# A planner that tracks every tile, and low weight halves kept in HBM, in a hybrid recurrent decoder step

## The chip, the cores and the metric

The kernel runs on one core of a Trainium2 chip. The metric is device time in microseconds for one execution. Three runs of the kernel before gave 3065.84, 3066.15 and 3074.48 us, median 3066.15. 

## The reference

One layer of a recurrent decoder, on 2048 prompt tokens and 32 sample tokens, model width 1024, all in float32:

```python
h = layernorm(x, emb_ln_g, emb_ln_b)
u = h @ w_in                       # 31 groups of 128 columns, for four mixers
y = concat(gated_deltanet(u), mamba2_ssd(u), hgrn2(u), mlstm(u))   # A, B, C, D
h1 = layernorm(alpha * h + y @ w_out, ln1)
out = layernorm(alpha * h1 + relu(h1 @ w_up) ** 2 @ w_down, ln2)   # d_ff 4096
```

The four mixers are causal recurrences. They are computed in chunks: inside a chunk by small matmuls with decay masks (A also solves a unit triangular system), and from chunk to chunk through a state matrix per head. The outputs are the tokens and all the final states.

## The kernel before

**Tiling.** The 2048 prompt tokens are four blocks of 512; the 32 sample tokens ride along in block 0 of the first projection and in block 2 of what follows, as 544 columns in two pieces of 272. The stages in PE's order: P(0) to P(3), the product with `w_in`; W(0), the product with `w_out`, placed inside P(3); then F(0) to F(3), the feed-forward part, with W(1) to W(3) inside the end of F(0) to F(2).

**Weight units.** A weight unit is 128 output columns by 512 rows, 256 KB. There are 832 in PE's order: 62 in each P, 16 in each W, 128 in each F (136 in F(3), where the last units are used twice for half the columns). Every float32 product is made of three passes in the faster `float32r` type: weights and activations are split into a high half (rounded) and a low half (the rest), and PE computes high x high, low x high and high x low. So a unit of 512 columns is 12 matmuls on PE, one of 544 columns 24. The weights are loaded again for every block, and split again: `wraw` is the load, ACT makes `whi` by a copy (`cpv`), and POOL or DVE makes `wlo = wraw - whi` (`w_split`, engine chosen by `tvp`). `w_pump`, called ahead of each unit, keeps loads up to five units ahead and splits up to three ahead. `wraw`, `whi` and `wlo` have four buffers each.

**Side chains.** Beside the products, the kernel weaves in generators: the evacuation and convolution of each group of `u` (`u_gen`), layer norms (`ln0`, `ln1`, `ln2`), loads of the mixers' output for `w_out` (`y_pre`), and two long state chains, `ma` for mixer A (PSUM tiles `pa`) and `mb` for B, C and D (PSUM tiles `pb`), 16 prompt chunks and one sample chunk in each. Every `yield` in such a generator ends a step; the next step's instructions are issued when the planner thinks that its inputs are ready. `R.tick`, called after every three product matmuls (six of 272 columns), decides.

**The planner.** The order of all engines is fixed when the program is built. `_Run` keeps a clock for each engine; `_Eng` wraps the engines and calls `cost` for each instruction. For an instruction of a side chain, `cost` lets it start at the latest of the engine's clock, the step's start, and the end of the chain's previous instruction, whatever that one touched. A DMA costs 0.55 us on SP's clock and is taken to land 2.5 us later. Buffers are not looked at. A step is issued when the chain's ready time is not more than `SLACK` = 0.03 us past PE's clock, and while DVE's and ACT's clocks are not over 2 us ahead of PE's.

**Queues.** Each engine takes its instructions in order, and a waiting one holds those behind it. All DMAs go out from SP's queue, in order as well. So a store that waits for its data, or a series of stores, holds the weight loads behind it.

## Time and profile before

| | |
|---|---|
| median of three runs | 3066.15 us |
| profiled run, span | 3058.42 us, 3056.6 us |
| PE busy, idle | 2889.3 us, 167.3 us |
| DVE, ACT, POOL busy | 2147.3, 1244.0, 1649.5 us |
| mean granted PE clock | 0.982 |
| moved by DMA | 407.10 MB, 133 GB/s on the mean |
| `wlo` made by POOL, by DVE | 740, 92 |
| last matmul of a state chain | 2396.9 us |

Stages begin at: P(0) 20.3 us, P(1) 260.0, P(2) 497.7, P(3) 732.1, F(0) 1041.4, F(1) 1603.0, F(2) 2175.6, F(3) 2672.1. The span runs from the first to the last instruction. PE's busy time is not its work alone: matmuls are pipelined, and where the granted clock is 0.5 they take twice as long and count as busy. All lines of the kernel's engine calls are one helper line (L253), DMAs another (L374), so groups are told apart by tiles.

### The profile page before, as it was taken

How to read it: one execution, taken by the hardware profiler on the slowest of the kernel's cores; microseconds unless marked ns; L12 is line 12 of the kernel's file. 1: busy time of each engine (PE TensorE's matmuls, PEld its weight loads, DVE VectorE, ACT ScalarE, POOL GpSimd, SP SyncE). 2: the span in 40 equal slices, each digit the busy share in tenths (PEclk: the TensorE clock that was granted, in tenths of full speed). 3: DMA queues.
4: the chain of work that ended last, by engine and by line, in shares of the span. 5: the costliest groups of instructions: out<-in, count | busy, mean ns of one | idle time of the engine just before them, and what ended most of it. 6: DMA issues, size and time to landing. Idle time of an engine off the chain costs nothing. (4 is left out here: it accounts for less than half of the span.)

```text
span 3056.6 us, 48030 instructions
## 1 busy us (share of the span) xinstructions
PE 2889.3 (95%) x16668; PEld 2484.1 (81%) x16668; DVE 2147.3 (70%) x4074; ACT 1244.0 (41%) x2645; POOL 1649.5 (54%) x1996
## 2 busy tenths in 40 slices
PE   7979999989999899999999999998989999999997
PEld 7978777778777688777877877888889999888886
DVE  6977887896986777777877766577787544474454
ACT  4654564654563533333344322233533222432222
POOL 5646775856665544654555536445363444444545
PEclk9989999999999999999999999999999999999999
DMA  6766465456466344454445424454333433333333
GB/s 189 97 180 183 119 197 174 123 153 200 108 166 185 116 135 129 130 162 126 141 127 145 128 85 139 125 167 138 108 120 108 130 90 89 110 117 97 97 95 98
DMA packets 361262, 407.10 MB, mean 133 GB/s; under 512 B 65468, under 2 KB 207804, under 8 KB 361020
## 3 DMA queue, kind: packets, MB, share of 16 engines
q1 hardware_dynamic: 361020, 404.04, 46.5%
q8 instruction: 132, 2.16, 0.3%
q14 instruction: 110, 0.90, 0.1%
HBM read 340.20 MB, written 63.72 MB: 132 GB/s over the span
## 5 line engine op out<-in xcount | busy, mean ns | idle before, releaser
L253 PE MATMUL pd<-g,whi 128*128 128x512 f32 (+2 forms) x8080 | 2238.4, 362 | 19.1 <-ACT g L253 8.8
L253 POOL TENSOR_TENSOR wlo<-wraw,whi 128x512 fp32r<-128x512 f32 x740 | 1040.3, 1413 | 1241.5 <-ACT whi L253 1074.1
L253 PEld LDWEIGHTS pd<-g,whi 128*128 128x128 f32 x8080 | 1393.9, 190 | 224.9 <-DVE g L253 10.9
L253 PE MATMUL pd<-g,wlo 128*128 128x512 f32 (+2 forms) x4040 | 1306.1, 354 | 14.7 <-POOL wlo L253 14.7
L253 PEld LDWEIGHTS pd<-g,wlo 128*128 128x128 f32 x4040 | 721.0, 191 | 107.1 <-POOL wlo L253 19.6
L253 ACT ACTIVATE whi<-wraw 128x512 fp32r<-128x512 f32 x795 | 487.6, 626 | 474.4 <-PE pd L253 254.9
L253 DVE TENSOR_TENSOR g<-g 128x512 fp32r<-128x512 f32 (+5 forms) x335 | 320.5, 961 | 171.7 <-ACT g L253 165.4
L253 ACT ACTIVATE g<-pd 128x512 f32<-128x512 f32 (+2 forms) x340 | 173.3, 528 | 533.6 <-PE pd L253 531.6
L253 DVE TENSOR_TENSOR g<-g,pd 128x512 f32<-128x512 f32 (+2 forms) x288 | 159.2, 570 | 209.1 <-PE pd L253 208.5
L253 ACT ACTIVATE g<-g 128x512 f32<-128x512 f32 (+4 forms) x358 | 218.8, 633 | 82.2 <-DVE g L253 46.9
L253 POOL TENSOR_TENSOR a<-nb,x 128x124 f32<-128x124 f32 (+30 forms) x496 | 193.5, 390 | 63.3 <-DMA nb<-ud32d 33.3
L253 POOL TENSOR_TENSOR x<-x,a 128x124 f32<-128x124 f32 (+30 forms) x496 | 193.8, 391 | 38.9
L253 DVE CAST g<-g 128x512 fp32r<-128x512 f32 (+1 forms) x154 | 157.8, 1025 | 25.5 <-POOL g L253 19.0
L253 POOL TENSOR_TENSOR g<-g 128x512 f32<-128x512 f32 (+3 forms) x83 | 121.7, 1472 | 36.9 <-ACT g L253 33.4
L253 ACT ACTIVATE b<-b 128x256 f32<-128x256 f32 (+3 forms) x201 | 81.2, 405 | 147.8 <-DVE b L253 147.1
L253 DVE TENSOR_TENSOR b<-laC 128x64 f32<-128x64 f32 (+2 forms) x474 | 125.2, 321 | 8.5 <-DMA laC<-UC 8.5
L253 DVE SCALAR_TENSOR_TENSOR g<-g,par 128x512 f32<-128x512 f32 (+1 forms) x128 | 124.8, 991 | 3.6 <-ACT g L253 3.6
L253 DVE SCALAR_TENSOR_TENSOR g<-g 128x512 f32<-128x512 f32 (+3 forms) x124 | 113.8, 926 | 7.2 <-ACT g L253 6.9
L253 DVE TENSOR_SCALAR g<-g 128x512 int32<-128x512 int32 (+7 forms) x137 | 86.9, 652 | 33.4 <-ACT g L253 32.5
L253 DVE TENSOR_TENSOR wlo<-wraw,whi 128x512 fp32r<-128x512 f32 x92 | 73.2, 796 | 52.6 <-ACT whi L253 52.1
L253 DVE TENSOR_TENSOR kzD<-laC,b 64x128 f32<-64x128 f32 (+1 forms) x228 | 103.1, 452 | 5.5 <-ACT b L253 3.9
L253 DVE BATCH_NORM_STATS2 bst<-g 128x6 f32<-128x512 f32 (+1 forms) x98 | 65.5, 680 | 40.5 <-ACT g L253 36.4
(2534 smaller groups left out, 2792.1 us busy)
## 6 DMA issues: line engine op xcount, KB each, us to landing
wraw<-in_w_dn_u_dram SPq DMA_DIRECT2D x264, 256.0 KB
wraw<-in_w_up_u_dram SPq DMA_DIRECT2D x256, 256.0 KB
wraw<-in_w_in_u_dram SPq DMA_DIRECT2D x248, 256.0 KB
nb<-ud32d SPq DMA_DIRECT2D x128, 256.0 KB
wraw<-in_w_out_u_dram SPq DMA_DIRECT2D x64, 256.0 KB
UC<-g SPq DMA_DIRECT2D x40, 256.0 KB
g<-in_x_prompt_dram SPq DMA_DIRECT2D x32, 256.0 KB
hTd<-g SPq DMA_DIRECT2D x32, 256.0 KB
```

The lines of the kernel that those rows point to most:

```text
L253: r = f(*a, **k)
```

## The change

**The planner** (`_Sim`, called by `_Run` and `_Eng`) records, for each tile, which part of it each instruction reads or writes, and when that ends. An instruction now starts when its own engine is free and the accesses that it really conflicts with have ended, with a delay per engine. A tile from a pool with 2 to 16 buffers starts when the accesses to the buffer's former tile have ended. DMAs take SP in order (0.42 us each), wait there for their data, share a wire priced by size, and land 1.6 us after. `SLACK` becomes -0.25.

**The low halves.** The first time a unit of `w_out`, `w_up` or `w_down` is split (for `w_in` the second time), the low half is also stored to HBM (`lod`), when the unit comes up on PE. Later blocks load it, right behind `wraw`, four units ahead of use, and do not compute it. `wraw` has three buffers now, `wlo` five. In the program, 206 halves are stored and 564 loaded; of the subtractions 240 stay on POOL and 28 on DVE. The number of PE's instructions is the same, and each side chain does the same steps.

**Starts.** `ln0(b)` starts when P(b-1) has reached unit group 8, and its stores of `hT` stand one to a step with paced early splits between them; `y_pre` waits until the end of the stage before is near; at the start, the fourth weight unit is loaded later.

```diff
-SLACK = 0.03
+SLACK = -0.25
+LN0_AT = 8
+KEEP = {"w_in_u": 2}
...
+class _Sim:
+    LAT = {"pe": 0.22, "act": 0.15, "dve": 0.15, "pool": 0.15, "dma": 0.0}
+    ISSUE = 0.42
+    PER_KB = 0.0035
+    LAND = 1.6
...
+    def enter(self, x):
...
+        ring = self.rings.setdefault(t.tag, deque())
+        if len(ring) >= meta.bufs:
...
+            old = ring[0]
+            ring.popleft()
+            self.floor[name] = max([e[5] + self.LAT[e[6]] for e in self.acc.pop(old)], default=0.0)
+        ring.append(name)
...
+    def need(self, eng, reads, writes):
+        t = 0.0
+        for w, xs in ((False, reads), (True, writes)):
+            for x in xs:
...
+                name, p0, p1, lo, hi, ps = self.region(x)
+                t = max(t, self.floor[name])
+                for a0, a1, al, ah, aw, end, ae in self.acc[name]:
+                    bank = ps and ae != eng and ae != "pe" and eng != "pe"
+                    if not bank and (not (w or aw) or a0 >= p1 or p0 >= a1 or al >= hi or lo >= ah):
+                        continue
+                    if ae == eng:
+                        if aw and eng in ("dve", "pool"):
+                            t = max(t, end + 0.1)
+                    else:
+                        t = max(t, end + self.LAT[ae])
+        return t
...
+    def run(self, eng, dur, reads, writes, pair=False):
+        c = self.clock
+        t0 = max(c[eng], self.need(eng, reads, writes))
+        if pair:
+            t0 = self.shared(eng, t0, dur)
+        c[eng] = t0 + dur
+        self.note(eng, t0 + dur, reads, writes)
+        return t0 + dur
+
+    def move(self, out, in_, extra=0.0):
+
+        c = self.clock
+        t0 = max(c["dma"], self.need("dmaq", (in_,), (out,)))
+        c["dma"] = t0 + self.ISSUE
...
+        self.wire = max(self.wire, t0 + self.ISSUE) + n / 1024 * self.PER_KB
+        end = max(self.wire, t0 + self.ISSUE) + self.LAND + extra
+        self.note("dma", end, (in_,), (out,))
+        return end
...
-    def cost(self, eng, dur, lat, pair=False):
-        g, c = self.cur, self.clock
-        t0 = c[eng]
-        if g is not self.main:
-            t0 = max(t0, g.base)
-            if g.last is not None:
-                t0 = max(t0, g.end - (lat if g.last == eng else 0.0) + (0.1 if g.last == eng and eng in ("dve", "pool") else 0.0))
...
+    wrp = ctx.enter_context(tc.tile_pool(name="wrp", bufs=3))
+    wlp = ctx.enter_context(tc.tile_pool(name="wlp", bufs=5))
...
     def w_get(i):
-        w = sb4.tile([128, 4, 128], F32, tag="wraw", name="wraw")
+        w = wrp.tile([128, 4, 128], F32, tag="wraw", name="wraw")
         dma(w, units[i])
-        raws[i] = w
+        lo = None
+        if keys[i] in lod:
+            lo = wlp.tile([128, 4, 128], F32R, tag="wlo", name="wlo")
+            dma(lo.bitcast(F32), lod[keys[i]])
+        raws[i] = (w, lo)
+
+    def lo_make(i, hi, eng):
+
+        w, lo = raws.pop(i)
+        if lo is not None:
+            return lo
+        lo = wlp.tile([128, 4, 128], F32R, tag="wlo", name="wlo")
+        tt(lo, w, hi.bitcast(F32), sub, eng())
+        key = keys[i]
+        made[key] = made.get(key, 0) + 1
+        if made[key] == KEEP.get(key[0], 1) and uses[key] > made[key]:
+            kept.append((i, key, lo))
+        return lo
+
+    def lo_keep(n):
+        while kept and kept[0][0] <= n:
+            _, key, lo = kept.popleft()
+            lod[key] = drp.tile([128, 4, 128], F32, name=f"lod{len(lod)}")
+            dma(lod[key], lo.bitcast(F32))
 
     def w_pump():
         cur = wst["cur"]
+        lo_keep(cur)
...
     def ln0(b):
+        while at["P"] < (b - 1, LN0_AT):
+            yield
...
         yield from _stagger([one(i) for i in range(CPB)], 5)
+        queue_set(("P", b), hT[b], TB)
         for k in range(8):
             dma(hTd[b][:, k, :], hT[b][k][:, 0:TB])
-        queue_set(("P", b), hT[b], TB)
-        for k in range(EARLY_P):
-            yield
-            split_next(("P", b))
+            yield
+            if k < EARLY_P:
+                while at["P"] < (b - 1, NPU - 2 * EARLY_P + 2 * k):
+                    yield
+                split_next(("P", b))
...
+        while at["F"] < (b - 1, FFB - 3) if b else at["P"] < (NB - 1, W0_AT - 10):
+            yield
```

What moves, at three places. First SP's queue in P(0), where the normalised tokens of block 1 are stored (`hTd`) between loads of state-chain operands (`laC`, `b` from `RB` and `UB`), stores of `u` (`UC`) and weight loads. Before:

```order
L374 DMA b_2593<-RB_181 128x4x128
L374 DMA b_2595<-RB_181 64x2x128 x2
L374 DMA b_2598<-UB_162 128x256
L374 DMA hTd_151<-g 128x512 x8
L374 DMA wraw<-in_w_in_u_dram 128x512
L374 DMA UC_163<-g 128x4x128
L374 DMA XC<-g 128x32
L374 DMA nb<-ud32d 128x1x512 x2
```

And of the change:

```order
L473 DMA b_2465<-UB_168 128x256
L473 DMA hTd_157<-g 128x512
L473 DMA wraw<-in_w_in_u_dram 128x512 x2
L473 DMA nb<-ud32d 128x1x512
L473 DMA UC_169<-g 128x4x128
L473 DMA XC<-g 128x32
L473 DMA wraw<-in_w_in_u_dram 128x512 x2
L473 DMA nb<-ud32d 128x1x512
L473 DMA hTd_157<-g 128x512
```

The eight stores stood in one series ahead of a weight load; now one store stands between loads.

Second, PE in a chunk of mixer D: from the transposes of its operands (`pb` from `con,laC`) to the product of queries and keys (`pb` from `laC,kzD`), with the weight products (`pd`) between. Before:

```order
L253 MATMUL pb__9729<-con,laC 128x128 x4
L253 MATMUL pd<-g,whi 128x512
L253 MATMUL pd<-g,wlo 128x512
L253 MATMUL pd<-g,whi 128x512 x2
L253 MATMUL pd<-g,wlo 128x512
L253 MATMUL pd<-g,whi 128x512 x2
L253 MATMUL pd<-g,wlo 128x512
L253 MATMUL pd<-g,whi 128x512 x2
L253 MATMUL pd<-g,wlo 128x512
L253 MATMUL pd<-g,whi 128x512
L253 MATMUL pa__9762<-con,laA 128x128 x4
L253 MATMUL pb__9772<-laC,kzD 128x128 x4
```

And of the change, at the same step:

```order
L342 MATMUL pb__8463<-con,laC 128x128 x4
L342 MATMUL pd<-g,whi 128x512
L342 MATMUL pd<-g,wlo 128x512
L342 MATMUL pd<-g,whi 128x512
L342 MATMUL pb__8479<-laC,kzD 128x128 x4
```

Twelve weight products stood between the two steps, three do now. Over the program, counted in the two orders, the weight products between successive steps of a state chain are fewer at 301 of 646 steps, more at 149 and as many at 196; the last step stands in weight unit 499 of 832, where it stood in unit 605.

Third, SP's queue where the feed-forward part goes from `w_down` to `w_up` units, while mixer A's solver reads its rows (`nb`). Before, in F(1):

```order
L374 DMA wraw<-in_w_dn_u_dram 128x512
L374 DMA nb<-ud32d 128x1x512 x2
L374 DMA wraw<-in_w_up_u_dram 128x512
L374 DMA out_sd_mem_dram<-g 128x260
L374 DMA wraw<-in_w_up_u_dram 128x512 x2
L374 DMA nb<-ud32d 128x1x512
L374 DMA wraw<-in_w_up_u_dram 128x512
```

And of the change, in F(1) too:

```order
L473 DMA wraw<-in_w_up_u_dram 128x512
L473 DMA wlo<-lod_13627 128x512
L473 DMA yTx<-b_19803 128x2x32
L473 DMA wraw<-in_w_up_u_dram 128x512
L473 DMA wlo<-lod_13650 128x512
L473 DMA nb<-ud32d 128x1x512
L473 DMA wraw<-in_w_up_u_dram 128x512
L473 DMA wlo<-lod_13693 128x512
L473 DMA laC<-UC_181 128x1024
```

Each weight load now has the load of its low half behind it, and the solver's and the chains' loads stand between such pairs.

More of the change, by code (lines that the diff above doesn't have):

```diff
@@ L171, in _adv, with op @@
             self.moved = self.moved or g.last is not None
[L173 to L195 removed]
+    def op(self, eng, end):
+        g = self.cur
         if g is not self.main:
             g.last = eng
[L198 removed]
+            g.end = max(end + self.sim.LAT[eng], g.end)
             g.ready = max(g.ready, g.end)
[L201 to L204 removed]
     def hold(self, us):
@@ L257, in call, with _ap @@
                 n *= x
-            self._run.cost(self._name, self._cost(fn, n, out, k), 0.22 if self._name == "pe" else 0.15, _pair(self._name, fn, a, k))
-            return r
-        return call
+            ins = [_ap(x) for x in list(a[1:]) + [v for key, v in k.items() if key != "out"] if hasattr(x, "tensor")]
+            if fn == "copy_predicated":
+                ins.append(_ap(out))
+            end = self._run.sim.run(self._name, self._cost(fn, n, out, k), ins, [_ap(out)], _pair(self._name, fn, a, k))
+            self._run.op(self._name, end)
+            return r
+        return call
+def _ap(x):
+    return x[:] if callable(x.ap) else x
 def _pe_cost(fn, n, out, k):
@@ L374, in dma @@
         nc.sync.dma_start(out=out, in_=in_)
-        R.cost("dma", 0.55, 2.5)
+        R.op("dma", R.sim.move(_ap(out), _ap(in_)))
     def A(out, in_, func, scale=1.0, bias=0.0):
@@ L525, with need @@
     raws, his = {}, {}
+    keys, uses, made, lod, kept = [], {}, {}, {}, deque()
+    def need(key, ap):
+        keys.append(key)
+        uses[key] = uses.get(key, 0) + 1
+        units.append(ap)
     def w_get(i):
-        w = sb4.tile([128, 4, 128], F32, tag="wraw", name="wraw")
+        w = wrp.tile([128, 4, 128], F32, tag="wraw", name="wraw")
         dma(w, units[i])
-        raws[i] = w
+        lo = None
[19 more added lines that the diff above has]
+            dma(lod[key], lo.bitcast(F32))
     def w_pump():
         cur = wst["cur"]
+        lo_keep(cur)
         while wst["nload"] < min(cur + 5, len(units)):
-            i = wst["nload"]
-            w_get(i)
+            w_get(wst["nload"])
             wst["nload"] += 1
@@ L753, in ln0_start @@
             if k == 5:
-                for i in range(4, 8):
+                for i in range(4, 7):
                     w_get(i)
-                wst["nload"] = 8
+                wst["nload"] = 7
         w_split()
@@ L1126, in dma_s @@
         nc.sync.dma_start(out=out, in_=in_)
-        R.cost("dma", 0.55, 0.0)
+        R.sim.move(_ap(out), _ap(in_))
     def dup(m, src):
@@ L2023, in fill_units, with half @@
     def fill_units():
-        W = lambda: [units.extend([t["w_out_u"][d, 0], t["w_out_u"][d, 1]]) for d in range(8)]
+        def half(name, u):
+            for k in range(2):
+                need((name, u, k), t[name][u, k])
+        W = lambda: [half("w_out_u", d) for d in range(8)]
         for b in range(NB):
@@ L2028, in fill_units @@
                     W()
-                units.extend([t["w_in_u"][u, 0], t["w_in_u"][u, 1]])
+                half("w_in_u", u)
         for b in range(NB):
@@ L2033, in fill_units @@
                 for j in range((4 if c == 0 else 3) + (1 if c + 1 < FFB else 0)):
-                    units.extend([t["w_up_u"][f, 0], t["w_up_u"][f, 1]])
+                    half("w_up_u", f)
                     f += 1
@@ L2038, in fill_units @@
                 for q in range(2 if b == NB - 1 and c == FFB - 1 else 1):
-                    units.extend(t["w_dn_u"][c, d] for d in range(8))
+                    for d in range(8):
+                        need(("w_dn_u", c, d), t["w_dn_u"][c, d])
     fill_units()
```

99 lines of the change are left out of this document (66 added, 33 removed).

## The prediction

> **What bounds the kernel now.** I read the engine totals first, then busy time by stretch. Stretches were cut where the side chains end: their last matmul (`pb__26253`) starts at 2396.9 us. Columns after the width: busy us and instructions of PE, PEld, DVE, ACT and POOL, then granted clock, DMA share, GB/s.
>
> ```profile
> PE 2889.3 (95%) x16668; PEld 2484.1 (81%) x16668; DVE 2147.3 (70%) x4074; ACT 1244.0 (41%) x2645; POOL 1649.5 (54%) x1996
> ...
> 0.00:2397.00 2397.00, 2247.31 (x12927) 1915.39 (x12927) 1812.77 (x3637) 1051.07 (x2298) 1329.65 (x1761) 0.98 0.50 142
> 2397.00:3056.60 659.60, 642.00 (x3744) 568.72 (x3742) 334.52 (x437) 192.90 (x347) 319.90 (x236) 0.99 0.35 102
> ...
> 0.00:20.30 20.30, 4.70 (x20) 3.21 (x20) 14.32 (x30) 6.91 (x13) 8.47 (x34) 1.00 0.60 204
> ...
> 260.00:497.70 237.70, 226.00 (x1124) 183.90 (x1123) 196.68 (x367) 135.76 (x287) 156.97 (x178) 0.97 0.54 160
> 497.70:732.10 234.40, 214.56 (x1034) 173.47 (x1033) 194.27 (x359) 130.31 (x269) 155.26 (x178) 0.98 0.54 162
> ...
> 1603.00:2175.60 572.60, 555.13 (x3221) 461.67 (x3221) 401.38 (x857) 196.31 (x436) 280.98 (x392) 0.99 0.45 130
> ...
> 2397.00:2672.00 275.00, 275.00 (x2040) 266.58 (x2038) 129.39 (x183) 84.49 (x158) 127.33 (x94) 1.00 0.35 103
> 2672.00:3010.00 338.00, 337.97 (x1484) 274.52 (x1484) 178.18 (x192) 93.50 (x163) 164.77 (x122) 1.00 0.35 101
> ```
>
> PE is the bound, and it does the same matmuls after the change. So only its waits and its clock can give anything. Without side chains (2397 to 3010 us) it never waits. With them, the **front**, it idles 2397.0 - 2247.3 = 149.7 us; 15.6 of that is the start, before the first product. So 134.1 us is on offer, plus the clock: at 0.98 over 2397 us, about 48 us of lost clock.
>
> Next, who ends PE's waits in the front (us, times, longest):
>
> ```profile
> PE pd L253 <- POOL wlo L253: 14.7, 10, 3.0
> PE pb__290 L253 <- ACT g L253: 13.7, 1, 13.7
> PE pd L253 <- ACT g L253: 11.4, 11, 3.9
> PE pb__2762 L253 <- ACT g L253: 7.8, 1, 7.8
> PE pb__24878 L253 <- DVE b L253: 4.6, 1, 4.6
> ...
> PE pd L253 <- DVE g L253: 4.2, 3, 1.6
> ```
>
> Low halves cost only 14.7. With the start (13.7) and the other `pd` waits (11.4, 4.2) taken off, some 106 us remain: single waits of chain steps (`pa`, `pb`), the largest 7.8. That one shows how they arise, in the timeline of three engines and the stretch behind it:
>
> ```profile
> 203.98 5.38 SPq L374 DMA_DIRECT2D hTd<-g  x8
> 209.41 0.52 SPq L374 DMA_DIRECT2D wraw<-in_w_in_u_dram  x1
> ...
> 212.85 0.63 ACT L253 ACTIVATE whi<-wraw 128x512 fp32r<-128x512 f32 x1 [10.43 <-DMA wraw<-in_w_in_u_dram]
> ...
> 215.91 0.77 PE L253 MATMUL pb__2762<-SB,b 128*128 128x128 f32 x2 [7.82 <-ACT g L253]
> ...
> 200.00:212.50 12.50, 8.10 (x66) 7.88 (x64) 2.39 (x4) 2.06 (x5) 2.68 (x2) 1.00 0.79 269
> 212.50:222.70 10.20, 6.79 (x29) 6.64 (x30) 5.55 (x11) 3.41 (x11) 2.79 (x2) 0.50 0.63 173
> ```
>
> Eight stores in a row keep SP busy; a weight load waits behind them; ACT, in order, waits 10.43 us for it with the chain's exponentials queued behind; PE reaches the chain's step and stands 7.82 us, then runs 10.2 us at half clock. The old planner prices a DMA at a fixed delay and never sees this queue.
>
> **The change, part by part.** *The planner.* Steps now wait for the tiles they touch, for ring buffers, for SP's order and the wire, rather than for everything their chain did before. The orders show both consequences. The eight stores are spread between weight loads. And the chains go faster: a state-chain step that had twelve products of cover has three, and the last chain row stands in weight unit 499 of 832, where it was 605. So 106 units move behind the chains: 36 of 512 columns, 70 of 544. Undisturbed units are priced by the chain of waits:
>
> ```profile
> 2397.22 243.76 PE pd L253 x1782
> ...
> 2701.69 308.14 PE pd L253 x1332
> ```
>
> At 24 matmuls a 544-column unit takes 3.28 us, at 12 a 512-column one 2.78. They carry 36 x 2.78 + 70 x 3.28 = 330 us. The front's own PE work becomes 2247 - 330 = 1917, what follows 330 + 660 = 990. Moving alone wins nothing: it thickens the chains in the front, so DVE there decides.
>
> *The low halves.* 564 of 832 units load theirs; 206 are stored once.
>
> ```profile
> L253 POOL TENSOR_TENSOR wlo<-wraw,whi 128x512 fp32r<-128x512 f32 x740 | 1040.3, 1413 | 1241.5 <-ACT whi L253 1074.1
> ...
> L253 DVE TENSOR_TENSOR wlo<-wraw,whi 128x512 fp32r<-128x512 f32 x92 | 73.2, 796 | 52.6 <-ACT whi L253 52.1
> L253 DVE CAST g<-g 128x512 fp32r<-128x512 f32 x118 | 118.5, 1004 | 20.1 <-POOL g L253 14.6 <-ACT g L253 2.4
> ...
> 2713.35 0.74 DVE L253 SCALAR_TENSOR_TENSOR g<-g,brs,lnb 128x512 f32<-128x512 f32 x1
> ...
> 2715.27 1.72 DVE L253 SCALAR_TENSOR_TENSOR g<-g,brs,lnb 128x512 f32<-128x512 f32 x1
> ...
> 2715.16 1.29 POOL L253 TENSOR_TENSOR wlo<-wraw,whi 128x512 fp32r<-128x512 f32 x1 [2.88 <-ACT whi L253]
> ...
> 215.69 0.42 DVE L253 CAST g<-g 128x512 fp32r<-128x512 f32 x1
> ```
>
> POOL loses 500 x 1.41 = 707 us, DVE 64 x 0.796 = 51. Neither sets the end by itself. What counts is the collision: the same DVE instruction takes 0.74 us alone and 1.72 when a POOL subtraction started before it, 0.98 more. The front now has 232 loaded halves (124 of `w_in`, 16 of `w_out`, 92 of the second feed-forward block); in the old proportion 740:92, 206 of them were POOL's. Freed DVE time is bounded by 0 and 206 x 0.98 = 202. The cast, 0.42 alone and 1.004 on average, was hit about (1.004 - 0.42)/0.98 = 60% of the time, so I take half: 101.
>
> The Trainium skill (SBUF — State Buffer, section "SBUF: two separate sides") says that the port pair of VectorE and GpSimd is an exclusive lock held for a whole instruction. By that rule the estimate is up to 206 x 1.41 = 290 us, and the sum below would stop at PE's bound. The measured pair agrees with a lock, but lost 0.98, not 1.41.
>
> *The price.* 770 more transfers of 256 KB, 202 MB on 404.
>
> ```profile
> L374 SPq DMA_DIRECT2D hTd<-g x32: 319/419/1183, 19.7 to 694.9; - x32
> ...
> q1 hardware_dynamic: 361020, 404.04, 46.5%
> ...
> 222.70:233.00 10.30, 8.92 (x67) 8.28 (x66) 6.36 (x11) 5.31 (x12) 8.87 (x14) 1.00 0.94 281
> ...
> SPq L374 <- DVE b L253: 331.6, 85, 12.5
> SPq L374 <- DVE g L253: 176.4, 71, 15.4
> ```
>
> On SP 770 x 0.42 = 323 us: with the old 1872 at the same price it issues for 1110 of 3000 us, no bound. On the wire 46.5% becomes 70% at the same price per byte. By stage: 162 GB/s plus 0.262 MB per 3.78 us (a `w_in` unit: 234.4/62) is 231, below the 281 already reached. So bandwidth costs nothing; lateness may. A load is issued four units, 11.1 us, ahead; the weight load above took 3.4 us from issue to use; 7.7 us is left for SP to be held, and SP's longest waits are 12.5 and 15.4. Per such event between 0 and 15.4 - 7.7 = 7.7 us; I put none in the forecast and five (38 us) in a rival. Raw buffers go from four to three: where halves are still made, SP waits one unit (2.78 us) longer; with a third of the ten waits above, 0 to 9 us. I take 0, inside the waits that stay.
>
> *Later starts.* The next block's embedding norm and the loads for `w_out` start later, with the same instructions. Cost 0 while five of eight splits still stand ahead of a block's first product, as they do; with that cover gone, a split is a cast (1.004) and a subtraction of like length, 2 us at each of three borders, 6 us. At the start the fourth weight unit is loaded after the first normalisation: 0 to 3.4 us; I take 0, since it is first used after two tiles' transposes.
>
> **The sum.** DVE in the front: 1813, less the moved units' share (330 x 129.39/275.00 = 155), less 51, less 101: 1506. Today DVE is busy 1813/2397 = 75.6% of the front, at most 194.27/234.40 = 82.9% of a stage. At 75.6% the front takes 1506/0.756 = 1992: PE then waits 75, start included, 59 instead of 134 otherwise. At 82.9% DVE would need 1817, less than PE's 1917 + 15.6, so PE binds at 1933. I take 75.6%: the planner's prices per instruction are the old ones, so it will not pack DVE tighter for free. 1992 + 990 = 2982. Clock: of 48 lost, the half-clock row shows 67% falling on busy PE (6.79/10.20), 32; with long waits down by the same 56%, 18 return: 2964. That is against the span 3056.6; its run took 3058.4 (+1.8), the median shown 3066.15 (+7.7 more). Forecast **2975 us**, own range 2935 to 3020.
>
> The Trainium skill (TensorE: Matmul & The Clock Gate, section "Part 1: The HAM clock gate") says that the clock halves after an idle window of about 3.4 us. By it, if only shorter waits stayed, all 32 would return: 2961. The half-clock row behind the 7.82 us wait agrees.
>
> **The rivals.**
> - *PE's floor.* The chains no longer make it wait: 1933 + 990 = 2923, with 18 to 32 of clock and 9.5 to the median 2900 to 2915. For it: 82.9% has been seen in two stages. Against: the planner still carries the same instruction prices and knows nothing of a halved clock.
> - *The low halves come late.* PE waits for `wlo` where SP was held: 2975 + 38 = 3013, up to 3050 with ten events.
> - *Waits per step stay.* The same 646 chain steps wait as long as before; only two thirds of the 14.7, the 7.8 and its clock go, some 20: about 3046. For it: counted in the orders, cover shrinks at 301 of the 646 steps and grows at 149.
> - *DVE becomes the bound: slower.* The chains' DVE work is squeezed into a shorter front. Without relief it is 1607, and at 75.6% the front takes 2126: 3116, in the median 3125. It decides once the front exceeds 3057 - 990 = 2067 us, that is at a DVE share under 73% with the relief, under 78% without.
>
> That the loads are not made is excluded: the order has them.
>
> **How the numbers follow.** Forecast 0.55, floor 0.10, late halves 0.08, waits stay 0.15 (0.09 still faster), DVE bound 0.12. This kernel's runs tell about 0.3% (9 us) from no change. Faster 0.55 + 0.10 + 0.08 + 0.09 = 0.82, same 0.06, slower 0.12. The range reaches from within the floor case to most of "waits stay": 2910 to 3055.
>
> **What would show it.** Right: the chains' last matmul near 1990 us; PE idle in the front near 75 us; DVE there near 1500 us, cast mean nearer 0.7 us; no ACT wait of 10 us behind `hTd`; granted clock 0.99. Wrong: PE waiting for `wlo` by DMA, a front over 2067 us, DVE above 1600 us in it, or PE idle past the chains' end.

## The result, and the profile after

The change made the kernel slower: 3141.62 us median of four runs (3130.42 to 3146.05) beside 3068.03 (3065.84 to 3074.48), ratio 1.0236, 95% interval 1.0217 to 1.0254. The forecast was 2975 us. The profiled run took 3141.96 us, its span 3140.0.

The last matmul of a state chain starts at 2161.7 us in the trace of after. First the page's line of the engines, then busy time by stretch (columns as in the prediction), cut there and, in the lower four rows, at the starts of P(2), P(3), F(0), F(1):

```profile
PE 2916.4 (93%) x16668; PEld 2500.6 (80%) x16668; DVE 1831.7 (58%) x4016; ACT 1258.3 (40%) x2658; POOL 880.6 (28%) x1487
...
0.00:2161.70 2161.70, 1952.90 (x10705) 1631.18 (x10706) 1479.97 (x3358) 958.93 (x2123) 834.93 (x1456) 0.96 0.66 196
2161.70:3140.00 978.30, 963.53 (x5966) 869.40 (x5964) 351.68 (x658) 299.37 (x535) 45.64 (x31) 0.99 0.61 190
...
526.20:796.00 269.80, 244.61 (x1227) 198.60 (x1228) 189.67 (x484) 150.49 (x329) 88.58 (x193) 0.95 0.74 226
796.00:1159.80 363.80, 320.35 (x1658) 263.88 (x1656) 236.08 (x570) 182.54 (x396) 116.00 (x262) 0.94 0.72 207
1159.80:1739.40 579.60, 558.00 (x3027) 453.32 (x3028) 411.07 (x894) 202.45 (x453) 265.85 (x421) 0.99 0.62 195
1739.40:2161.70 422.30, 372.83 (x2002) 310.24 (x2001) 251.36 (x664) 142.23 (x339) 84.80 (x217) 0.94 0.61 182
```

Behind the chains all is as forecast (978 us, 990 predicted). The front took 2162 us in place of 1992. PE is idle there for 2161.7 - 1952.9 = 208.8 us, where 75 were forecast and 149.7 stood before, and its clock is 0.96: about 89 us lost (from the unrounded clock) where 48 were. Yet DVE is busy for 1480 us only, 68.5% of the front. The stages with loaded halves, P(2), P(3) and F(1), run at 0.94 to 0.95 with 25 to 50 us of idle PE each. F(0), which computes its halves of `w_up` and `w_down`, runs at 0.99 with 21.6 us of idle in 579.6.

Who ends PE's waits (us, times, longest), from the first rows of that view of after:

```profile
...
PE pb__19825 L342 <- DVE b L342: 10.9, 1, 10.9
...
PE pd L342 <- POOL wlo L342: 8.0, 11, 1.3
PE pa__22018 L342 <- DVE a L342: 7.1, 1, 7.1
...
PE pa__10177 L342 <- DVE a L342: 7.0, 1, 7.0
PE pa__19096 L342 <- DVE a L342: 6.6, 1, 6.6
PE pa__20218 L342 <- DVE a L342: 6.2, 1, 6.2
PE pa__21135 L342 <- DVE a L342: 6.0, 1, 6.0
PE pa__9164 L342 <- DVE a L342: 6.0, 1, 6.0
```

The `pa` rows are one step of mixer A's chunks: the transposes of the solved matrix (`pa<-con,a`), right behind the solver that POOL runs row by row. Summed over the trace, PE waits 60.3 us there in 12 chunks, where the kernel before waited 16.9 in 13. What is late is not DVE. The chain of waits that ends in `pa__19096` (start, us, what):

```profile
1712.71 8.08 DMA nb<-ud32d
1720.84 0.09 issue
1720.93 0.33 POOL a L342
...
1724.61 8.99 DMA nb<-ud32d
1733.64 0.09 issue
1733.73 0.30 POOL a L342
...
1736.92 6.78 DMA nb<-ud32d
1743.74 0.09 issue
1743.83 0.23 POOL a L342
...
1745.29 0.22 POOL x L342
1745.53 1.73 DVE a L342
1747.31 1.12 PE pa__19096 L342 x4
```

The solver reads its 32 rows from HBM in eight transfers, with two buffers (`nb`): each of the last six is issued when POOL has used up a buffer. Each takes 7 to 9 us from its issue to POOL's first use, and POOL's work on one is 3 to 4 us. The new planner counts on 0.42 + 0.9 + 1.6 = 2.9 us for such a transfer (issue, 256 KB on the wire, landing), so it lets PE come for the result too soon. The stretches around the end of this chain:

```profile
1739.00:1745.00 6.00, 1.72 (x10) 1.22 (x8) 0.00 (x0) 0.00 (x0) 2.24 (x11) 0.91 0.65 213
1745.00:1752.40 7.40, 5.09 (x22) 4.30 (x23) 6.60 (x12) 3.35 (x7) 1.63 (x3) 0.62 0.26 77
1752.40:1765.00 12.60, 12.60 (x83) 10.31 (x82) 3.05 (x8) 4.71 (x10) 1.08 (x2) 1.00 0.58 163
```

DVE and ACT do nothing either in the 6 us of the first row, and in the next 7.4 us the mean clock is 0.62. The Trainium skill (TensorE: Matmul & The Clock Gate, section "Part 1: The HAM clock gate") has the clock halve after an idle window of about 3.4 us; this 6.58 us wait agrees. Nine waits of this step are longer than 3 us. They hold 56.5 us, and in the 15 us behind each another 20.9 us of clock are lost in all (11.5 more are lost within the waits, where no matmul runs). In the kernel before one wait of this step is longer than 3 us, with 1.7 us of clock behind it. So the step's waits grew by 43.4 us and the clock behind the long ones by 19.2, together 63 us, beside the 83.4 by which the spans differ. PE's other waits in the front sum to 148.5 us (132.8 before); the forecast needed them to fall.

The longest row above, 10.9 us at `pb__19825`, has another cause. The chain that ends in it:

```profile
1807.51 9.44 DMA laC<-UB
...
1817.01 4.13 DMA wraw<-in_w_dn_u_dram
...
1821.25 0.63 ACT whi L342
1821.88 0.31 ACT b L342
...
1823.79 0.39 PE pb__19825 L342 x2
```

The weight load is issued the moment that `laC` has landed, eight places ahead of it in SP's queue. ACT stands 15.9 us for that unit, with the chain's instruction (`b`) queued behind, and PE stands in turn. In this program SP's transfers share eight completion semaphores in rotation, and an issue waits until the transfer eight places ahead, which has the same one, has landed. Such waits cost SP 50.2 us in 61 cases in the kernel before, and 200.1 us in 227 in this one; with the halves alone (e2 below) 183.8, with the planner alone (e1) 61.3. Most often it is a row transfer that holds the queue. In the trace of before, and then of after:

```profile
SPq L374 <- DMA nb<-ud32d: 47.5, 28, 4.6
```

```profile
SPq L473 <- DMA nb<-ud32d: 139.4, 73, 4.6
```

Neither planner counts transfers in flight. How much of the loss comes this way, beside the waits behind the solvers, no run separates.

### The profile page after: what moved, and what is told of

Read it like the earlier page. It is cut to its first block, busy times and chain, and to the rows that moved or that the text cites. A ratio compares the mean times of both kernels' runs of the same rounds, so it can differ in the third digit from the quotient of the medians.

```text
span 3140.0 us, 48365 instructions
## 1 busy us (share of the span) xinstructions
PE 2916.4 (93%) x16668; PEld 2500.6 (80%) x16668; DVE 1831.7 (58%) x4016; ACT 1258.3 (40%) x2658; POOL 880.6 (28%) x1487
## 4 chain that ended last, share of the span: by engine, by line
PE 45%; DMA 10%; DVE 3%; POOL 3%; issue 3%; SPq 1%; ACT 1%; POOLq 0%; DVEq 0%; ACTq 0%
PE pd L342 39%; DMA nb<-ud32d 5%; DMA wraw<-in_w_dn_u_dram 2%; DVE g L342 1%; DMA wraw<-in_w_up_u_dram 1%; SPq L473 1%; POOL wlo L342 1%; POOL a L342 1%; POOL x L342 1%; DVE b L342 1%; DVE a L342 1%; DMA wraw<-in_w_out_u_dram 1%; DMA lod<-wlo 0%; DMA laC<-UB 0%; DMA laC<-UD 0%
## 5 line engine op out<-in xcount | busy, mean ns | idle before, releaser
L342 PE MATMUL pd<-g,whi 128*128 128x512 f32 (+2 forms) x8144 | 2272.4, 364 | 22.3 <-DVE g L342 9.6
L342 ACT ACTIVATE whi<-wraw 128x512 fp32r<-128x512 f32 x826 | 511.0, 628 | 740.4 <-PE pd L342 321.7
L342 POOL TENSOR_TENSOR wlo<-wraw,whi 128x512 fp32r<-128x512 f32 x240 | 332.3, 1392 | 488.2 <-ACT whi L342 434.6
L342 DVE TENSOR_TENSOR g<-g 128x512 fp32r<-128x512 f32 (+5 forms) x360 | 278.2, 776 | 304.4 <-ACT g L342 295.9
L342 ACT ACTIVATE g<-pd 128x512 f32<-128x512 f32 (+1 forms) x326 | 164.2, 522 | 453.6 <-PE pd L342 448.3
L342 POOL TENSOR_TENSOR g<-g 128x512 f32<-128x512 f32 (+3 forms) x58 | 81.8, 1413 | 667.3 <-DMA g<-hTd 318.1
L342 ACT ACTIVATE g<-g 128x512 f32<-128x512 f32 (+5 forms) x325 | 200.8, 634 | 61.8 <-DVE g L342 48.9
L342 POOL TENSOR_TENSOR g<-g,lng 128x512 f32<-128x512 f32 (+1 forms) x18 | 28.4, 1578 | 439.3 <-ACT g L342 439.3
L342 DVE SCALAR_TENSOR_TENSOR g<-g,pd 128x512 f32<-128x512 f32 (+1 forms) x80 | 45.0, 583 | 101.2 <-PE pd L342 95.9
L342 DVE CAST g<-g 128x512 fp32r<-128x512 f32 (+1 forms) x187 | 100.1, 535 | 6.3 <-ACT g L342 1.1
L342 DVE BATCH_NORM_STATS2 bst<-g 128x6 f32<-128x512 f32 (+1 forms) x98 | 65.7, 684 | 61.3 <-ACT g L342 56.9
```

Source lines behind the costliest of these rows:

```text
L342: r = f(*a, **k)
```

## The experiments

Two theories were set against each other first: **P**, the planner expects its DMA data too early, and **T**, the halves' transfers make all loads late. From the first four runs came **N**: what is priced too early, and what decides, is the solver's row transfers alone.

The table has all runs. "Behind solvers" is the sum of PE's waits at the step above. "Clock lost" is one minus the granted clock, times the front. "Plan" is where PE's clock in the kernel's own planner ends when the program is built; it is no measurement. Kernels were run in groups beside the kernel before, whose medians were 3070 to 3077 us; ratios are against the one of the group. Idle, clock and waits are those of the one profiled run; that of e7 was the fastest of its four, 3008.9 us, where the others took 3025 to 3033.

```
run                           us     ratio (95% interval)     front   idle  clock lost  behind solvers  plan
before                      3068.0                             2397    150      48          16.9       3078
after                       3141.6  1.0236 (1.0217..1.0254)    2162    209      89          60.3       2886
e1  planner alone           3117.1  1.0143 (1.0109..1.0178)    2361    190      55          15.4       2860
e2  halves alone            3088.4  1.0043 (1.0026..1.0059)    2374    174      73          36.0       3069
e3  all landings 5.0 us     3137.9  1.0200 (1.0178..1.0223)    2308    192     106          44.0       3264
e4  rows +4 us              3097.3  1.0063 (1.0039..1.0088)    2209    183      61          30.4       2890
e5  e1 with rows +4 us      3044.8  0.9899 (0.9882..0.9917)    2291    141      34           6.8       2859
e6  before, 3 raw buffers   3097.4  1.0070 (1.0055..1.0085)    2436    174      53          23.3       3078
e7  rows +8 us              3025.9  0.9824 (0.9792..0.9856)    2501    118      34           2.5       2883
e8  two row trips           3008.1  0.9771 (0.9755..0.9788)    2005    115      48           8.9       2876
e9  e7, 4 raw buffers       3023.2  0.9825 (0.9811..0.9840)    2498    122      31           4.2       2868
e10 e9 without halves       3058.2  0.9941 (0.9924..0.9957)    2571    145      46           9.3       2869
e11 e7, old margin          3024.4  0.9835 (0.9820..0.9850)    2512    122      41           4.3       2888
e12 e7, all landings 5.0    3288.0  1.0692 (1.0675..1.0710)    2817    278     208          43.4       3589
e13 e7, weights 5.0         3122.6  1.0152 (1.0131..1.0174)    2607    183      96           6.9       3052
e14 e7, all but weights 5.0 3111.4  1.0118 (1.0095..1.0141)    2599    173      80           5.8       3219
e15 before, rows 9.5 us     3302.2  1.0734 (1.0712..1.0756)    2830    273     199          33.1       3419
e16 e2 with rows 9.5 us     3220.9  1.0472 (1.0451..1.0493)    2754    223     185          22.0       3403
e17 before, two row trips   3106.9  1.0120 (1.0100..1.0140)    2409    178      73          13.5       3055
e18 e1, two row trips       3083.2  1.0050 (1.0031..1.0068)    2296    161      46           8.0       2860
```

### Each half of the change by itself

The planner alone, e1:

```diff
-KEEP = {"w_in_u": 2}
+KEEP = {"w_in_u": 99, "w_out_u": 99, "w_up_u": 99, "w_dn_u": 99}
```

> The tile-tracking planner with its -0.25 slack, and every low half computed as before (none stored, none loaded; three raw and five low buffers as in the change). Theory P (the planner expects a DMA's data about 2.9 us after it is issued, while the trace of the change has solver rows landing after 7.9 us at the median and weights after 5.8 to 7.3; so chain steps are placed too early, with or without the low halves): not faster than before, 3060 to 3150 us. Rival T (the 770 extra transfers of the low halves make every load late): clearly faster than before, 2980 to 3040 us.

The halves alone, e2, put the old planner back: its `cost`, `shared`, `sync` and `SLACK` = 0.03, the old `ln0` and `y_pre`.

> The old planner, with the low halves stored and loaded as in the change. Theory P: POOL and DVE are relieved and the old cover of the chain steps stays, so faster than before or the same, 3010 to 3070 us. Rival T: slower than before, 3090 to 3150 us.

Both lose: 1.4% and 0.4%. e1 is in P's range, e2 between the two (3070 and 3090), so neither theory holds by itself. In e1 the loss is spread (the step behind the solvers holds 15.4 us of 190 idle); in e2 that step is the largest, 36.0 us. Neither run is quite one half: both have the change's three raw buffers, which cost the kernel before 20 us by themselves (e6 below), more than e2's 15 us; and e1 has the later starts, which no run takes apart from the planner.

### The price of transfers

All landings, e3:

```diff
-    LAND = 1.6
+    LAND = 5.0
```

> The change, with one number of the planner raised: a DMA's data is expected 5.0 us after the wire instead of 1.6, about 6.3 us after issue. Theory P: waits on the solver's rows and on chunk loads fall, 3000 to 3070 us, at least 70 us below the change. Rival T: the transfers are as many, so 3110 to 3150 us.

Only the solver's rows, e4:

```diff
+    def dma_x(out, in_):
+        nc.sync.dma_start(out=out, in_=in_)
+        R.op("dma", R.sim.move(_ap(out), _ap(in_), 4.0))
...
-                    dma(nb[q]...
+                    dma_x(nb[q]...
```

> The change, with the landing of the solver's rows (nb) alone expected 4 us later. Theory P in its narrow form (the solver's rows alone carry the loss): 3050 to 3085 us, with the waits of mixer A's transposes gone. In its wide form (all loads are expected too early): 3090 to 3125 us. Rival T: no change, 3130 to 3150 us.

e3 won nothing (3138 us, in T's range). e4 won 44 us and halved the waits behind the solvers. Its 3097 us are in the range that was given to P's wide form, 12 us above that of the narrow one, which said that these waits would be gone. What speaks for the narrow form is that e4 won and e3, which raises the same price with all others, did not. N was then put to four runs. First the planner alone with the same edit, e5:

> The change's planner with all low halves computed (as in the planner-alone run, 3117 us) and the eight row transfers of each solver priced 4 us longer, as in the run that brought the whole change from 3142 to 3097 us. Theory N (the planner's harm is the price of the solver rows: they land 6 to 8 us after their issue and it counts on 2.9): the gain is the same 30 to 50 us as with the halves, so 3070 to 3087 us, and TensorE's wait behind the solvers falls below 15 us from 15.4. Theory S (the planner's harm is spread over many steps because it takes a step when it expects it ready, with no margin): at most 15 us are won, 3102 us or more, and the waits on kzD, wlo and whi of 13 to 26 us each stay.

It won 72 us, more than N expected, and was the first version faster than the kernel before. Only some 9 us of that went behind the solvers; the rest of the gain is idle and clock spread over the front. Next the raw buffers, e6:

```diff
+    wrp = ctx.enter_context(tc.tile_pool(name="wrp", bufs=3))
+    wlp = ctx.enter_context(tc.tile_pool(name="wlp", bufs=5))
...
-        w = sb4.tile([128, 4, 128], F32, tag="wraw", name="wraw")
+        w = wrp.tile([128, 4, 128], F32, tag="wraw", name="wraw")
...
-        lo = sb4.tile([128, 4, 128], F32R, tag="wlo", name="wlo")
+        lo = wlp.tile([128, 4, 128], F32R, tag="wlo", name="wlo")
```

> The kernel before with one change, three buffers for raw weight units and five for low halves in place of four and four. If the missing raw buffer is a large part of what planner and halves lose alone (weights ask for their transfer later, casts wait for them), this is 10 us or more slower, 3084 us or more, with ScalarE's waits for raw units up. If it is nothing, as the prediction took (0 of 0 to 9 us), it stays within 5 us of the kernel before.

One raw buffer less costs the kernel before 0.7%, some 20 us. The old planner does not look at buffers, and each engine's instructions stand in the same order in both traces, so this is the buffer and not another order. Its rows for ACT's wait for raw units and PE's for low halves, in e6,

```profile
ACT whi L253 <- DMA wraw<-in_w_in_u_dram: 94.0, 41, 10.5
...
PE pd L253 <- POOL wlo L253: 22.7, 23, 3.7
```

were 57.1 and 14.7 before. Then 8 us on the rows, and on the store of the rows ahead of them, e7:

```diff
-        R.op("dma", R.sim.move(_ap(out), _ap(in_), 4.0))
+        R.op("dma", R.sim.move(_ap(out), _ap(in_), 8.0))
...
-            dma(ud32d, ud.rearrange("p h r -> p (h r)"))
+            dma_x(ud32d, ud.rearrange("p h r -> p (h r)"))
```

> The whole change with the solver's row transfers priced 8 us longer (in place of 4 in the run of 3097 us), and the store of the rows ahead of them too. Theory N (an expectation that is too early by 4 to 5 us per round trip is the loss): at 4 us the error is nearly gone, so 8 us wins little more by the row trips, but the store was still counted too early, once for each solver: 3080 to 3100 us. If a margin of any size helps because other steps are late too, it goes on falling, to 3050 to 3080 us. If chains delayed past need cost more than waits, it rises to 3105 to 3125 us, and the chains end later than at 4 us.

3026 us, 1.8% faster than before, and below all three ranges; nearest is the second, that more margin goes on helping. The planner now counts on 10.9 us for a trip, where in after the median is 8.0 and nine in ten take under 10.6 (the 85 trips of the table further down). What the later store wins by itself was not run apart. The front of e7, and the first rows of PE's waits:

```profile
0.00:2501.40 2501.40, 2383.95 (x14116) 2055.12 (x14117) 1632.12 (x3661) 1101.22 (x2390) 872.99 (x1471) 0.99 0.69 204
...
PE pd L342 <- DVE g L342: 15.9, 9, 5.3
PE pb__296 L342 <- ACT g L342: 13.7, 1, 13.7
PE pd L342 <- ACT g L342: 9.6, 11, 2.2
```

No `pa` step behind a solver is left among the first. The chains now end at 2501 us, later than in the kernel before (2397), and still it is faster: an early end of the chains is worth nothing by itself. POOL's wait for the rows has not gone, only PE's. Its row in after and in e7:

```profile
POOL a L342 <- DMA nb<-ud32d: 411.2, 85, 51.1
```

```profile
POOL a L342 <- DMA nb<-ud32d: 468.5, 57, 53.1
```

POOL waits longest where it has nothing else to do, so this row alone says nothing about the time.

### The trips taken away

e8 makes only the first two trips of each solver, with the planner's prices as the change has them:

```diff
-                if k % 4 == 3:
-                    fetch(k // 4 + NBUF)
...
-                tt(tf[:, :, 0:w_], nb[k // 4][:, k % 4, :, k + 1:], ...
+                tt(tf[:, :, 0:w_], nb[k // 4 % NBUF][:, k % 4, :, k + 1:], ...
```

> The whole change with only the first two of a solver's eight row transfers; from the ninth row on the solver reads the first eight rows again, so the solved matrix is another one and the work the same. Theory N: six of eight trips of each solver are gone, and with them the planner's error; TensorE's wait behind the solvers falls from 60 us to under 15 us, and the time comes to 3040 to 3080 us. If the waits there are the last of several chains that are all as late (casts, kzD, laC), others take their place, and it stays at 3105 us or more.

3008 us, below what N gave; the waits behind the solvers fell from 60.3 to 8.9 us. Less stands in the queue as well: 96 of the 128 row transfers are gone, and SP's waits for the transfer eight places ahead fell from 200.1 to 76.3 us. So e8 shows what the trips cost, not by which of the two ways. Its two stretches, cut at its last chain matmul:

```profile
0.00:2005.00 2005.00, 1889.70 (x10598) 1590.95 (x10599) 1470.23 (x3343) 941.63 (x2092) 885.60 (x1469) 0.98 0.67 195
2005.00:3008.40 1003.40, 988.70 (x6072) 889.63 (x6070) 362.58 (x677) 306.40 (x548) 45.59 (x31) 0.99 0.62 193
```

The same without trips for the kernel before (e17) and for the planner alone (e18):

> The kernel before with only the first two of a solver's eight row transfers (from the ninth row on it reads the first eight again, another solved matrix and the same work). Beside the whole change without those trips, 3008 us. If the trips were the one thing on which the change turns from a gain into a loss, the kernel before wins little by losing them, since TensorE waits only 17 us behind its solvers: 3045 to 3070 us, and the change without trips is 40 to 60 us faster than this, as predicted of it with trips. If the trips hold up the kernel before as much as the change, it falls to 3005 to 3030 us, and the change is worth nothing in itself.

> The planner alone, all low halves computed (3117 us), with only the first two of the eight row transfers. If the planner's loss was the price of the trips, it falls by 60 us or more, to 3010 to 3055 us, and what is left to the 3008 us of the whole change without trips is what the halves are worth. If the planner alone loses by steps that are taken too early elsewhere, it stays above 3085 us.

The kernel before does not gain from losing its trips, it loses 1.2%: its order changes, and PE's waits for low halves grow from 14.7 us to

```profile
PE pd L253 <- POOL wlo L253: 31.8, 17, 5.7
```

So without the trips the change is 3008 against 3107 us, about 3%; this is more than the 40 to 60 us expected only because the kernel before got slower, by its new order. Against the kernel before with its trips it is 2.3%. The planner alone falls by 34 us, between the two outcomes given (60 us or more; no lower than 3085): its loss is partly the trips, partly something that no run here names. Three raw buffers are in it too.

### Combinations of the mended version

e9 gives e7 its fourth raw buffer back and loads the halves three units ahead; e10 is e9 without halves; e11 is e7 with `SLACK` = 0.03.

```diff
-    wrp = ctx.enter_context(tc.tile_pool(name="wrp", bufs=3))
-    wlp = ctx.enter_context(tc.tile_pool(name="wlp", bufs=5))
+    wrp = ctx.enter_context(tc.tile_pool(name="wrp", bufs=4))
+    wlp = ctx.enter_context(tc.tile_pool(name="wlp", bufs=4))
...
-        lo = None
-        if keys[i] in lod:
-            lo = wlp.tile([128, 4, 128], F32R, tag="wlo", name="wlo")
-            dma(lo.bitcast(F32), lod[keys[i]])
-        raws[i] = (w, lo)
+        raws[i] = (w, None)
+        if i - 1 in raws and keys[i - 1] in lod:
+            lo = wlp.tile([128, 4, 128], F32R, tag="wlo", name="wlo")
+            dma(lo.bitcast(F32), lod[keys[i - 1]])
+            raws[i - 1] = (raws[i - 1][0], lo)
```

> The run with row trips priced 8 us longer (3026 us) with four raw weight buffers and four for low halves, as before the change has them, in place of three and five; a stored half is loaded three units ahead and not four. Theory R (the raw buffer that the change gives up costs here what it cost the kernel before, 20 us): 3003 to 3015 us, with ScalarE's waits for raw units and TensorE's for high halves (6.4 us) down. If the new planner's margins already cover it, 3020 to 3032 us. If the low halves come too late with three units of lead, TensorE's wait for low halves behind a transfer shows and it is 3035 us or more.

> The change's planner without any stored halves, row trips priced 8 us longer, buffers four and four as before: the planner alone with both suspected faults mended. Theory N with R: the planner alone fell from 3117 to 3045 us with 4 us on the row trips; the rest of the price and the raw buffer win 15 to 30 us more, 3012 to 3030 us. If so the stored halves, which take some 80 us off VectorE and GpSimd in the front, win nothing against the run beside it (within 10 us of it). If the halves are worth their transfers, this one stays at 3035 us or more.

> The run with row trips priced 8 us longer with the old margin in the rule that takes a chain's next step (0.03 us after it is ready in place of 0.25 us ahead of it). If steps taken early were part of the loss, TensorE's many short waits on kzD and con,b (32 us together) fall and the time is 3000 to 3015 us; if the price of the transfers was all that mattered, 3018 to 3032 us.

e7, e9 and e11 cannot be told apart. In e9 a new wait shows, which stood in no earlier run:

```profile
PE pd L342 <- DMA wlo<-lod: 18.1, 12, 6.6
```

With three units of lead the low halves do come late. A gain from the fourth raw buffer does not show beside it: ACT's waits for raw units sum to 274 us in e7 and 316 in e9, PE's for high halves to 6.4 and 10.3. e10 says what the halves are worth once the rows are priced: 3058 against 3023 us, 35 us. That refutes its expectation (within 10 us). The margin (e11) is worth nothing that can be measured. Its expectation has the sign the wrong way round: a step is taken when its ready time is at most `SLACK` past PE's clock, so 0.03 takes steps 0.28 us earlier than -0.25, not later.

### Late prices

e3 and e7 contradict each other unless a late price of other transfers does harm. e12 is both edits together; e13 puts 5.0 us on loads of weights and halves alone, e14 on all others; the solver's rows keep e7's price in both.

> The run with row trips priced 8 us longer, and with every transfer's landing at 5.0 us in place of 1.6, as in the run that raised all landings alone and stayed at 3138 us. If a longer landing for all transfers does harm of its own (there it hid the gain of 3.4 us more on the row trips), this one is far above 3026 us, 3060 us or more. If it was only that 3.4 us were too little on the row trips, it stays within 15 us of 3026 us.

> The run with row trips priced 8 us longer (3026 us), and only the loads of weights and of stored halves priced at a landing of 5.0 us in place of 1.6. Theory W (the harm of late prices for all transfers, 3288 us, is the planner's pace: it believes that TensorE stands waiting for weights, its own clock ends at 3052 us here against 2883 us without and 3589 us with all landings late, and so it puts the chains' steps between fewer matmuls than the chip then needs): a clock a little above the chip's 3007 us does a little harm, 3035 to 3090 us. If a late price of any transfer simply sends steps later, nothing is lost: 3015 to 3035 us.

> The run with row trips priced 8 us longer, and all transfers but the weights and stored halves priced at a landing of 5.0 us. By theory W what counts is the planner's own clock, which ends at 3219 us here, above the chip's: 3090 to 3200 us, slower than the run with late weights. If the late weights alone were the harm of the 3288 us, this one stays at 3015 to 3040 us.

The harm is real: 3288 us with all landings late, 3123 with the weights', 3111 with the others'. The front of e12:

```profile
0.00:2817.20 2817.20, 2539.53 (x14516) 2192.82 (x14516) 1662.81 (x3722) 1105.82 (x2394) 859.51 (x1468) 0.93 0.63 184
```

278 us of idle and 208 of lost clock. In all three the planner's own clock ends later (3052 to 3589 us, 2883 in e7): the plan itself has become long. But theory W ordered them by that clock, and e13 with the earlier one is not the faster; e13 is above both outcomes given for it (3090 at most). So that these later prices make the order worse is shown; by which rule of the planner is open. Last, the same mend in the old planner, without and with the halves (e15, e16):

```diff
+    def dma_x(out, in_):
+        nc.sync.dma_start(out=out, in_=in_)
+        R.cost("dma", 0.55, 9.5)
...
-                    dma(nb[q]...
+                    dma_x(nb[q]...
```

> The kernel before with its old planner, and the row trips priced at 9.5 us of latency in place of 2.5. Theory N says the old planner has the same fault, only covered by its slower, rougher prices (TensorE waits 17 us behind the solvers): 15 to 30 us are won, 3045 to 3060 us, and TensorE's wait behind the solvers goes below 5 us. If the old planner's order is bound by something else, it stays within 8 us of before.

> The stored and loaded halves with the old planner (3088 us) and the row trips priced at 9.5 us of latency in place of 2.5. Theory N: the halves lengthen each row trip, and what they lost was this wait (36 us behind the solvers); with it priced, they are worth what they take off VectorE, and it is 3010 to 3040 us, as fast as the new planner with the same price, so that the new planner itself brings nothing. If the access-tracking planner is worth its own part, this stays 20 us or more above 3023 us.

Both are far slower, 7.3% and 4.7%, against N's forecast of a gain. The old planner starts each instruction of a chain after the end of the one before, and has no account of buffers. So a trip that is issued two buffers ahead is charged in full, eight times per solver; its plan grew from 3078 to 3419 us. That this is why it got slower is argued, not shown. N therefore holds for the new planner only.

### The length of a row trip

From the traces, median time from the issue of a row transfer to the POOL instruction that it let go, over the transfers for which POOL stood idle:

```
kernel                       halves   trips   median us
before                       made        22     6.5
e1  planner alone            made        46     6.8
e5  e1 with rows +4 us       made         9     7.0
e6  before, 3 raw buffers    made        34     6.8
e2  halves alone             loaded      76     7.9
after                        loaded      85     8.0
e9  e7, 4 raw buffers        loaded      56     7.5
after, in F(0)               made        21     7.3
after, in P(2), P(3), F(1)   loaded      57     9.4, 8.5, 8.0
```

So theory T was right in a part: with the halves' transfers beside it a trip takes some 1 to 1.5 us longer (e2 against e1, after against before). Within after it is longest in the stages that load halves, and all nine long waits behind the solvers are in these three.

## Why the prediction was wrong

**PE is the bound, its matmuls are the same, 106 units move.** Right. The back took 978 us (990 forecast), and PE runs 12927 - 10705 = 2222 instructions fewer in the front, which fits the 36 x 12 + 70 x 24 = 2112 matmuls of the moved units.

**DVE in the front 1506 us.** Right: 1480, and the row of the cast

```profile
L342 DVE CAST g<-g 128x512 fp32r<-128x512 f32 (+1 forms) x187 | 100.1, 535 | 6.3 <-ACT g L342 1.1
```

shows 0.535 us on the mean (0.546 for the 128x512 form alone) where 0.7 was forecast and 1.004 stood. The relief from the collisions was put too low, on the safe side. Two of its terms do not fit together: the 51 us take all 64 of DVE's missing subtractions off the front, while 206 of 232 for POOL leaves DVE 26; with 64, POOL's are 168 and half the relief is 82 us, not 101.

**"At 75.6% the front takes 1506/0.756 = 1992."** This step failed. It took PE's waits as set by DVE's share, and the front came to 2162 at a share of 68.5%, with DVE idle in the waits. What makes PE wait is a step placed before its data, and the data came from a chain of row transfers that no share of a busy engine shows: 60.3 us of PE's 208.8 are waits behind the solvers, and with the rows alone (and their store) priced 8 us later 2.5 us are (e7). With six of the eight trips gone the front is 2005 us at 73.3% and the back 1003: 3008 us, where the forecast was 1992 + 990 (less 18 of clock). That the front comes within 13 us is in part luck: PE idles 115 us there where 75 were forecast, and the clock loses 48 as it did before where 30 were forecast, but more units moved behind the chains than were counted (10598 instructions are left in the front; 12927 less 2112 would be 10815). The spans fell by 48 us, about half of the 92 that the sum promised. So without the trips the direction was right and the waits were still sized too small.

**"Bandwidth costs nothing; lateness may"**, with lateness put into a rival and looked for at `wlo`. The first half failed in its effect: each row trip became 1 to 1.5 us longer, and SP waited 200 us in place of 50 for transfers eight places ahead. The second half looked at the wrong load. PE's wait for low halves is 8.7 us in after, none of it ended by a transfer; the loads that were late were the solver's, and once, with 10.9 us on PE, a raw unit. The prediction quoted that the weights' load took 3.4 us from issue to use, and never measured the rows (6.5 us in the trace of before), nor set either beside the planner's new 1.6 us landing. The trace of before had what was needed. The old planner's price was hardly longer (0.55 + 2.5 = 3.05 us), but it charged each trip behind the end of the chain's instruction before it, and the change took this cover away. That the cover is why the old price did little harm is argued, not shown.

**Raw buffers from four to three, 0 of 0 to 9 us.** Too small where it was measured: 20 us in the kernel before (e6). In the mended version it does not show apart from the halves' shorter lead (e9). ACT waits longer for raw units in after as well: for those of `w_in` 57.1 us in 26 waits before, for those of `w_down` 37.2 in 20, and now

```profile
ACT whi L342 <- DMA wraw<-in_w_in_u_dram: 166.0, 64, 8.3
...
ACT whi L342 <- DMA wraw<-in_w_dn_u_dram: 98.8, 53, 15.9
...
PE pd L342 <- ACT whi L342: 7.1, 5, 2.5
```

By the lowest row PE waits only 7.1 us for high halves directly. But chain instructions queue behind ACT's waits, as in the 10.9 us above; what more of them reaches PE that way no run separates. The wait of 10.4 us behind the eight stores is gone, as forecast; the longest for a unit of `w_in` is 8.3, for one of `w_down` 15.9.

**Clock: 18 us return.** 41 more were lost. Of the 89 now lost, 20.9 us lie in the 15 us behind the nine long waits at the solvers and 11.5 within them.

**The rivals.** "DVE becomes the bound" had the time (3125) and its sign (front over 2067 us), but its mechanism is refuted: DVE is busy 1480 us, so its time is luck. "Waits per step stay" was nearer in kind: outside the solvers' step PE's waits in the front are 148.5 us, after 132.8. None named the solver's trips. Three of the signs that the prediction offered showed it: PE idle in the front, the front's length and the clock.

**What the change is worth by itself** hangs on that price: with the rows 8 us later it is 1.8% faster than before, and e10 and e9 divide that into some 18 us for the planner, with its starts, and 35 for the halves.

## What to carry to other kernels

Before a planner's constants are trusted, set each against the issue-to-use time of that very transfer in the trace: here 2.9 us were counted on and 8.0 taken, eight times for each solver, and the price of this transfer and of the store ahead of it turned +2.4% into -1.8%. A price near the median was not enough: 6.9 us gave 3097 us, and 10.9 with the later store gave 3026; no run stands between. Raise such a price only where the trace shows a wait behind it; later prices for all transfers on top of it made the same kernel 9% slower (e12 against e7), and in a planner that charges every step of a chain in turn the later row price cost 7% (e15). A busy share does not tell how long a dependent chain is, so count its round trips when a change speeds up everything beside it. And count the transfers in flight as well as their bytes: here SP's waits for the transfer eight places ahead grew fourfold, below a bandwidth already reached.

## What the runs showed of the hardware

A row transfer of 256 KB, broadcast from HBM, took 6.5 us from issue to use at a DMA share of 0.50 in the front and 8.0 at 0.66. The bandwidths (142 and 196 GB/s) were below the 281 that a stretch of the kernel before had reached.

On SP's queue an issue waited for the landing of the transfer eight places ahead, which has the same completion semaphore: 50.2 us in all with 1872 transfers, 200.1 with 2642.

Nine waits of about 6 us on PE, 56.5 us together, had 20.9 us of lost clock in the 15 us behind them. And programs with the same matmuls, which differ in prices, buffers and where the halves come from, gave from 3023 to 3302 us; the kernel before got slower by both edits of its row trips (e15, e17), of which one takes work away. So one version that is slower says little about the idea in it.
